# A three-branch scan backbone: each engine's queue put into the order of the kernel's own list schedule

## The chip, the core and the metric

The kernel runs on one core of one Trainium2 chip. The core has five engines with a queue each: TensorE (PE in the profile, its weight loads PEld), VectorE (DVE), ScalarE (ACT), GpSimd (POOL), and SyncE (SP), from whose queue every transfer between the device's memory and the core's own is issued here. An engine takes its instructions in the order in which they stand in its queue; an instruction that waits for a result holds up all that stand behind it. The metric is the device time of one execution in microseconds (us), lower is better.

## The reference

There are two layers over 256 context and 512 latent tokens of width 1024. Each layer projects the normed, modulated tokens once, runs three kinds of scan over them in both directions, and projects the joined results back:

```python
u_lat = rmsnorm(h_lat, norm_w[l]) * (1.0 + scale[:, None]) + shift[:, None]
...
(z_c, xbc_c, dt_c, q_c, k_c, v_c, gg_c, lr_c, u5_c, sg_c) = split_in_proj(u_ctx @ w_in[l])
(z_l, xbc_l, dt_l, q_l, k_l, v_l, gg_l, lr_l, u5_l, sg_l) = split_in_proj(u_lat @ w_in[l])
ssd_c, ssd_l = ssd_branch(...)
gla_c, gla_l = gla_branch(...)
s5_c, s5_l = s5_branch(...)
out_lat = jnp.concatenate([ssd_l, gla_l, s5_l], axis=-1) @ w_out[l]
h_lat = h_lat + gate[:, None] * out_lat
```

The SSD branch (16 heads, a convolution before it) and the GLA branch (4 heads) are linear-attention scans over chunks of 128 and 64 tokens; the S5 branch is a complex diagonal recurrence. Each runs forward and backward, context first, and hands its last state to the latent scan. The second layer gives out latent tokens alone.

## The kernel before

Everything lies channel by token: 128 channels on the partitions, up to 768 tokens along them. A projection of 128 output channels (`proj`, matmuls of L497 for the latent and L499 for the context tokens; `L691` for v) loads a weight block `wr`, splits it into a high part `wh` (ACT) and a low part `wl` (POOL, every third time DVE, L421), and sums 24 matmuls of 512 columns in a PSUM tile `pl` (and 24 of 256 columns in `pc`). The S5 output gate (L1008, L1010) and the output projection (L1044, L1046) are built alike. These matmuls, 5088 of the 6920, are called projections below; the others belong to the scans, norms and modulations.

The program is traced layer by layer in this order: modulation and norm; a small projection for dt and the decay of the scans; S5 input (`s5_in_maps` L351 to L359, matmuls L599), S5 recurrence on DVE (L631 to L634), S5 output (L672 to L674); q, k and v; the GLA heads (L765 to L793) and, in layer 0, the gate's share of the modulation (`mod_tiles`, L202); the gates (`spill_gate`, evicted by DVE at L516); GLA's norm (L808); twelve convolution tiles (`conv_tile`, L838 to L847); the SSD scan in six steps for each of two head groups; the z gates; the S5 output gate; `ssd_norm` (its first matmul is L955); the half of the output projection that takes GLA and S5 (`spilled_part`), and last the half that takes SSD.

An SSD step has three parts. `decay` loads rows of `acsD` into 128 partitions (L887, 1 MB) and makes the decay matrix with eight pairs of ACT and DVE instructions (L897 to L900); `within` multiplies it by the tokens (L908, L910); `between` carries the state: POOL weighs the tokens (L926) and decays the state (L936), PE makes the update (L931), DVE adds it (L937), and the part of the output that comes from the state is loaded for (L919), made (L917, L922) and added by POOL (L923). Each group has one work tile, `bA` or `bB`, so a load for the next step waits until the step before has read its rows.

Nothing in the kernel's text orders the engines. It is traced under `tile.TileContext(nc, schedule_with_timeline_sim=True)`: a scheduler goes through the traced instructions, gives out the buffers of the tile pools and sets the order of every queue, by the traced order as priority and durations from a model of its own.

Of the kernel before, what the change touches and what calls it, by code (L numbers as in the profile page):

```python
# [2 lines left out]

# [6 lines left out]
F32R = mybir.dt.float32r  # L10
# [27 lines left out]
STEPS = [(0, 1), (1, 0), (2, 5), (3, 4), (4, 3), (5, 2)]  # L38


@with_exitstack
def hybrid_backbone_kernel(
    ctx: ExitStack,
# [15 lines left out]
    V, S, G, PE = nc.vector, nc.scalar, nc.gpsimd, nc.tensor  # L59
# [8 lines left out]

    def T(tag, shape, bufs, dt=F32):
        uid[0] += 1  # L70
        return sb.tile(shape, dt, tag=tag, bufs=bufs, name=f"{tag}_{uid[0]}")

    def cv(n=NT):
        return T("cv", [128, NT], 3)[:, :n]

    def ev(n=NT):
        return T("ev", [128, 776], 2)[:, :n]

    def cs(n=1024):
        return T("cs", [128, 1024], 3)[:, :n]  # L80
# [13 lines left out]

    def m12():
        return T("m12", [128, 3072], 1)

    def ps(n=512, p=128):
        uid[0] += 1
        return psp.tile([128, 512], F32, tag="ps", bufs=3, name=f"ps_{uid[0]}")[:p, :n]  # L100
# [26 lines left out]
    def pcol(name, i=0, n=1):  # L127
        a = PAR[name][0] + i
        return P_[:, a : a + n]
# [351 lines left out]
    def layer(l, u):  # L481
# [216 lines left out]


        g4 = m12()  # L700
        gh = [g4[:, NT * i : NT * i + NT] for i in range(4)]
        wk = big("bB")
# [152 lines left out]
        def ssd_prep(g):  # L855

            if g == 0:
                t = m12()
                xtok = lambda c: t[:, 512 * c : 512 * c + 512]
            else:  # L860
                t = [cs() for _ in range(3)]
                xtok = lambda c: t[c // 2][:, 512 * (c % 2) : 512 * (c % 2) + 512]
            xts.append(xtok)
            for c in range(6):
                pt = ps()
                for i in range(4):
# [272 lines left out]
    hx, acc = layer(0, u)  # L1139
# [10 lines left out]
    hx, acc = layer(1, u)  # L1150
# [6 lines left out]
    for k in range(8):  # L1157
        o = hx[:, k, LC:NT]
        if k in POOL_FIN:
            G.tensor_tensor(o, o, rstd, MUL)  # L1160
        else:
            V.scalar_tensor_tensor(o, o, pcol("fnw", k), rstd, MUL, MUL)
        dma(outT[128 * k : 128 * k + 128], o)


def lay_out(np, x, c, ctx, c_ctx, norm_w, mod_w, mod_b, w_in, w_out, ssd_conv_w, ssd_conv_b, ssd_a_log,
# [77 lines left out]
```

## Time and profile before

| | |
|---|---|
| median of 3 runs | 1715.96 us (1715.52 to 1718.87) |
| profiled execution | 1718.59 us |
| its span, first to last instruction | 1716.9 us |
| busy: PE, DVE, ACT, POOL | 1415.7, 1209.7, 681.8, 596.5 us |
| mean granted TensorE clock | 0.906 of full |
| transfers | 234.42 MB, mean 137 GB/s |

Busy time is the time in which at least one instruction of an engine runs. Matmuls overlap, and where the clock is at the lower of its two levels the same work takes longer, so a busy PE is not a PE at full rate. [...]

### The profile page before, as it was taken

The numbers are of one execution on the slowest core, as the hardware profiler recorded it, in microseconds if no ns is written. First come the engines' busy times: TensorE is split into PE (matmuls) and PEld (weight loads), VectorE is DVE, ScalarE is ACT, GpSimd is POOL, SyncE is SP. The second block draws the span as 40 slices with busy tenths as digits, with TensorE's granted clock in tenths as the row PEclk, the third lists the DMA queues.
The fourth block names the chain that finished last, engine by engine and source line by source line (L and its number), as shares of the span: only waits on it lengthen the run. The fifth ranks groups of instructions, "written<-read, shape, count | busy, mean of one in ns | idle before, by whom it ended". The sixth has DMA issues, their size and how long they took to land.

```text
span 1716.9 us, 23372 instructions
## 1 busy us (share of the span) xinstructions
PE 1415.7 (82%) x8536; PEld 1141.4 (66%) x8536; DVE 1209.7 (70%) x2184; ACT 681.8 (40%) x1220; POOL 596.5 (35%) x492
## 2 busy tenths in 40 slices
PE   3879887787998988666899887996889888967786
PEld 1657776685877867455776655794679777745564
DVE  7957679824679778889913694559974986688742
ACT  3313242443335554544211241234254435545452
POOL 3201344312331244545222211144343232655454
PEclk8889998869998998888999988998988998988998
DMA  8564432246232235443485428722235333344542
GB/s 306 134 176 124 132 102 77 89 138 214 76 120 93 74 136 165 147 128 120 160 300 181 119 68 206 226 76 89 90 120 148 95 119 97 120 132 151 174 146 92
DMA packets 137147, 234.42 MB, mean 137 GB/s; under 512 B 31688, under 2 KB 72136, under 8 KB 137032
## 3 DMA queue, kind: packets, MB, share of 16 engines
q1 hardware_dynamic: 137032, 232.93, 43.9%
q8 instruction: 67, 1.10, 0.3%
q14 instruction: 48, 0.39, 0.1%
HBM read 188.25 MB, written 44.63 MB: 136 GB/s over the span
## 4 chain that ended last, share of the span: by engine, by line
DVE 32%; PE 28%; DMA 19%; issue 7%; ACT 6%; POOL 4%; SPq 1%; DVEq 0%; ACTq 0%; POOLq 0%
PE pl L497 7%; PE pl L1044 5%; DMA bB<-acsD 5%; DMA bc<-lpD 4%; PE pc L499 3%; DMA bA<-acsD 3%; DMA cs<-in_mod_w 3%; DVE xy L845 2%; PE pc L1046 2%; ACT bA L121 2%; DVE xy L633 2%; DVE xy L634 2%; PE pl L691 1%; DMA cs<-in_s5cb 1%; DVE bB L898 1%
## 5 line engine op out<-in xcount | busy, mean ns | idle before, releaser
L497 PE MATMUL pl<-hl,wh 128*128 128x512 f32 (+1 forms) x1184 | 409.5, 412 | 36.6 <-DVE ev L516 21.3
L421 POOL TENSOR_TENSOR wl<-wr,wh 128x1024 fp32r<-128x1024 f32 (+1 forms) x82 | 211.7, 2583 | 486.6 <-ACT wh L121 473.0
L497 PEld LDWEIGHTS pl<-hl,wh 128*128 128x128 f32 (+1 forms) x1184 | 225.4, 194 | 95.1 <-DVE ev L516 23.4
L497 PE MATMUL pl<-hl,wl 128*128 128x512 f32 (+1 forms) x592 | 241.7, 409 | 11.3 <-DVE wl L421 10.0
L121 ACT ACTIVATE wh<-wr 128x1024 fp32r<-128x1024 f32 (+1 forms) x122 | 127.7, 1046 | 236.4 <-PE pc L499 79.2
L499 PE MATMUL pc<-hl,wh 128*128 128x256 f32 (+1 forms) x864 | 211.5, 315 | 4.4 <-DVE ev L516 3.2
L499 PEld LDWEIGHTS pc<-hl,wh 128*128 128x128 f32 (+1 forms) x864 | 160.8, 212 | 20.5 <-issue 9.3
L497 PEld LDWEIGHTS pl<-hl,wl 128*128 128x128 f32 (+1 forms) x592 | 114.7, 194 | 40.0 <-DVE wl L421 11.1
L499 PE MATMUL pc<-hl,wl 128*128 128x256 f32 (+1 forms) x432 | 133.6, 310 | 0.0
L1044 PE MATMUL pl<-hl,wh 128*128 128x512 f32 x256 | 88.3, 421 | 15.8 <-ACT hl L121 4.6
L499 PEld LDWEIGHTS pc<-hl,wl 128*128 128x128 f32 (+1 forms) x432 | 90.9, 210 | 4.6 <-issue 3.2
L121 ACT ACTIVATE ev<-pl 128x512 f32<-128x512 f32 (+1 forms) x96 | 51.3, 534 | 94.7 <-PE pl L691 31.5
L121 ACT ACTIVATE bB<-bB 128x512 f32<-128x512 f32 (+4 forms) x40 | 45.7, 1143 | 98.0 <-DMA bB<-acsD 57.8
L845 DVE SCALAR_TENSOR_TENSOR xy<-ev,par_sb,xy 128x512 f32<-128x512 f32 (+1 forms) x112 | 81.6, 756 | 0.8
L691 PE MATMUL pl<-wh,hl 128*128 128x256 f32 x384 | 73.5, 291 | 0.0
L1044 PEld LDWEIGHTS pl<-hl,wh 128*128 128x128 f32 x256 | 50.4, 202 | 31.4 <-ACT hl L121 6.3
L691 PEld LDWEIGHTS pl<-wh,hl 128*128 128x128 f32 x384 | 61.1, 195 | 4.7 <-ACT bB L121 3.0
L421 DVE TENSOR_TENSOR wl<-wr,wh 128x1024 fp32r<-128x1024 f32 x40 | 54.5, 1361 | 11.4 <-ACT wh L121 11.2
L691 PE MATMUL pl<-wl,hl 128*128 128x256 f32 x192 | 55.3, 291 | 5.7 <-POOL wl L421 5.7
L1008 PE MATMUL pl<-hl,wh 128*128 128x512 f32 x128 | 48.2, 443 | 11.3 <-ACT cv L121 8.0
L1044 PE MATMUL pl<-hl,wl 128*128 128x512 f32 x128 | 53.2, 415 | 3.2 <-DVE wl L421 2.0
L121 ACT ACTIVATE bA<-bA 128x512 f32<-128x512 f32 (+2 forms) x30 | 23.5, 784 | 79.6 <-DMA bA<-acsD 59.1
(476 smaller groups left out, 3409.8 us busy)
## 6 DMA issues: line engine op xcount, KB each, us to landing
wr<-in_wblk SPq DMA_DIRECT2D x80, 512.0 KB
wr<-in_wout SPq DMA_DIRECT2D x32, 512.0 KB
hl<-in_mod_w SPq DMA_DIRECT2D x20, 512.0 KB
bA<-acsD SPq DMA_DIRECT2D x10, 1024.0 KB
bB<-acsD SPq DMA_DIRECT2D x10, 1024.0 KB
bc<-lpD SPq DMA_DIRECT2D x16, 512.0 KB
clD<-cs SPq DMA_DIRECT2D x64, 128.0 KB
cs<-clD SPq DMA_DIRECT2D x32, 256.0 KB
```

The lines of the kernel that those rows point to most:

```text
L121: return S.activation(out, in_, f, **kw)
L421: (eng or (V if wcount[0] % 3 == 0 else G)).tensor_tensor(wl, wr, wh.bitcast(F32), SUB)
L497: PE.matmul(p_l[:m], lhs, u[k][:, ui, LC:NT], start=st, stop=sp)
L499: PE.matmul(p_c[:m], lhs, u[k][:, ui, 0:LC], start=st, stop=sp)
L633: V.tensor_tensor(dst, dst, tr[:, 0, :n], ADD)
L634: V.tensor_tensor(dst, dst, tr[:, 1, :n], ADD)
L691: PE.matmul(p, u[k][:, ui, 128 * c : 128 * c + 128], ws[k // 4][wi][:, 256 * (k % 4) : 256 * (k % 4) + 256], start=n == 0, stop=n == 23)
L845: V.scalar_tensor_tensor(ac, raw[:, o + k : o + k + n], pcol("cw", w0 + k), ac, MUL, ADD)
L898: V.scalar_tensor_tensor(rf[:, h, :], rbw[:, h, :], rb[:, ih : ih + 1], rf[:, h, :], SUB, MIN)
L1008: PE.matmul(p_l, lhs, yg5[k][:, ui, LC:NT], start=n == 0, stop=n == 11)
L1044: PE.matmul(p_l, lhs, rhs[kk][:, ui, LC - t0 : NT - t0], start=st, stop=sp)
L1046: PE.matmul(p_c, lhs, rhs[kk][:, ui, 0:LC], start=st, stop=sp)
```

## The change

At the end of the trace the kernel calls a function of its own, `order_queues`. It makes a record for each traced instruction (`Step`): its queue, what it reads and writes, a duration from a formula for its engine and kind, and a lag until others may use the result. From the accesses it works out which instruction waits for which, and then goes through simulated time: whenever a queue is free, it takes the instruction that was traced first among those whose inputs have landed, if the pools have room for the tiles that it opens. It counts a DVE instruction with two streams from the core's memory and any POOL instruction but a memset as users of one port that only one may hold. At the end it adds an edge between each two neighbours of a queue, so that the scheduler that still runs afterwards has to keep this order. No instruction is added, removed or moved to another engine: both programs have the same 6920 matmuls, 748 transfers and 35 loads of ACT's function tables.

```diff
+    def cost(self):
...
+        if self.queue == "PE":
+            n, self.lag = cols(self.writes[0]), 150
+            if self.reads[0].dtype == F32R:
+                self.time = n * (0.443 if n >= 512 else 0.469)
+            else:
+                self.time = 2 * max(0.85 * n + 8, 118 if cols(self.reads[1]) > 64 else 75)
+        elif self.queue == "DVE":
+            scan = any(a.tensor.name.startswith("sm_") for a in self.reads)
+            self.time, self.lag = 60 + 2.28 * n if scan else ((120 if psum else 62) + n) / 0.96 + 25, 90
+            self.port = not psum and sum(cols(a) > 1 for a in self.reads) >= 2
+        elif self.queue == "Pool":
+            a, b = {"TensorTensor": (100, 2.18), "Memset": (90, 0.6), "TensorScalarPtr": (200, 1.6)}.get(self.kind, (150, 1.6))
+            self.time, self.lag, self.port = a + b * n, 120, self.kind != "Memset"
+        elif self.queue == "Activation":
+            self.time, self.lag = 120 + 0.88 * n, 120
...
+            rate = 190 if small >= 1024 else 120 if small >= 512 else 60
+            if any(s == 0 for s, _ in self.reads[0].ap):
+                rate = 95
+            self.time, self.lag, self.flow = 450, 2000, self.bytes / rate
...
+def order_queues(tc):
...
+    while count < len(steps):
...
+        for q in queues:
+            while free[q] <= now and heaps[q]:
+                skipped, s = [], None
+                while heaps[q] and len(skipped) < 60:
+                    n = heapq.heappop(heaps[q])
+                    if fits(steps[n]):
+                        if not (steps[n].port and port > now):
+                            s = steps[n]
+                            break
...
+    info = mybir.DependencyInfo(mybir.DependencyClass.NoSync, mybir.DependencyReason.DATA)
+    for q in queues:
+        for a, b in zip(done[q], done[q][1:]):
+            tc.add_manual_dep(b.ins, a.ins.name, info, reason="order of the queue")
...
         dma(outT[128 * k : 128 * k + 128], o)
+    order_queues(tc)
```

In the changed file a line of the kernel stands 197 lines lower: L497 is L694, L931 is L1128, and so on. Three places show how the orders differ.

PE, layer 1, SSD steps. `pl` is a z gate's projection; `ps` of L931 (L1128) is the update of an SSD state, `bA` and `bB` the two groups. Before, 24 projections and one transpose stand between the update into ps_11197 and the next one, into ps_11205; these are the last of them:

```order
L497 MATMUL pl_12073<-hl_8010,wl_12070 128x512
L497 MATMUL pl_12073<-hl_8015,wh_12069 128x512
L928 MATMUL pa_11249<-ident,bc_10753 128x128
L497 MATMUL pl_12073<-hl_8015,wh_12069 128x512
L497 MATMUL pl_12073<-hl_8015,wl_12070 128x512
L497 MATMUL pl_12073<-hl_8020,wh_12069 128x512 x2
L497 MATMUL pl_12073<-hl_8020,wl_12070 128x512
L497 MATMUL pl_12073<-hl_8025,wh_12069 128x512 x2
L497 MATMUL pl_12073<-hl_8025,wl_12070 128x512
L497 MATMUL pl_12073<-hl_8030,wh_12069 128x512 x2
L497 MATMUL pl_12073<-hl_8030,wl_12070 128x512
L931 MATMUL ps_11205<-bA_11163 128x512
```

In the changed order this is the whole stretch between the same two updates:

```order
L1128 MATMUL ps_11190<-bB_11164 128x512
L1128 MATMUL ps_11197<-bA_11163 128x512
L1125 MATMUL pa_11249<-ident,bc_10753 128x128
L694 MATMUL pl_11898<-hl_8030,wl_11895 128x512
L694 MATMUL pl_11933<-hl_7995,wh_11929 128x512
L1125 MATMUL pa_11257<-ident,bc_10753 128x128
L694 MATMUL pl_11933<-hl_7995,wh_11929 128x512
L694 MATMUL pl_11933<-hl_7995,wl_11930 128x512
L694 MATMUL pl_11933<-hl_8000,wh_11929 128x512 x2
L694 MATMUL pl_11933<-hl_8000,wl_11930 128x512
L1128 MATMUL ps_11205<-bA_11163 128x512
```

There are 7 projections between the two updates now, of gates that were traced earlier; the 24 of before stand further back.

POOL, the same steps. L926 and L936 are `between`'s, `wl` (L421) splits a weight block for a projection. Before:

```order
L936 TENSOR_TENSOR bB_11164<-bB_11164,dts_8183 128x512
L421 TENSOR_TENSOR wl_12070<-wr_12067,wh_12069 128x1024
L926 TENSOR_TENSOR bB_11164<-cs_11120,wf_8184 128x512
L926 TENSOR_TENSOR bA_11163<-m_1072_10656,wf_8184 128x512
L936 TENSOR_TENSOR bB_11164<-bB_11164,dts_8183 128x512
L926 TENSOR_TENSOR bA_11163<-m_1072_10656,wf_8184 128x512
L421 TENSOR_TENSOR wl_12160<-wr_12157,wh_12159 128x1024
L926 TENSOR_TENSOR bB_11164<-cs_11120,wf_8184 128x512
L421 TENSOR_TENSOR wl_12201<-wr_12198,wh_12200 128x1024
L926 TENSOR_TENSOR bB_11164<-cs_11121,wf_8184 128x512
```

After, at the end of the SSD steps:

```order
L1133 TENSOR_TENSOR bA_11163<-bA_11163,dts_8183 128x512
L1123 TENSOR_TENSOR bB_11164<-cs_11122,wf_8184 128x512
L618 TENSOR_TENSOR wl_12035<-wr_12032,wh_12034 128x1024
L618 TENSOR_TENSOR wl_12070<-wr_12067,wh_12069 128x1024
L1133 TENSOR_TENSOR bB_11164<-bB_11164,dts_8183 128x512
L1123 TENSOR_TENSOR bB_11164<-cs_11121,wf_8184 128x512
L1120 TENSOR_TENSOR xy_10216<-xy_10216,bB_11164 128x4x128 x2
L1133 TENSOR_TENSOR bB_11164<-bB_11164,dts_8183 128x512
L1120 TENSOR_TENSOR xy_10216<-xy_10216,bA_11163 128x4x128 x2
L1120 TENSOR_TENSOR xy_10216<-xy_10216,bB_11164 128x4x128 x2
L618 TENSOR_TENSOR wl_12160<-wr_12157,wh_12159 128x1024
L618 TENSOR_TENSOR wl_12201<-wr_12198,wh_12200 128x1024
```

The splits for two z gates (wl_12035, wl_12070) and for the S5 output gate (wl_12160, wl_12201), which stood among the first SSD steps, stand near the last ones or behind them.

PE, layer 1, S5 output (L672 to L674, tiles `pa`). Before, it stands among gate projections and a GLA head (L765):

```order
L497 MATMUL pl_10299<-hl_8020,wl_10296 128x512
L765 MATMUL ps_9629<-bB_9451,m_932_9450 128x128
L765 MATMUL ps_9630<-bB_9451,m_932_9450 128x128
L765 MATMUL ps_9629<-bB_9451,m_932_9450 128x128
L765 MATMUL ps_9630<-bB_9451,m_932_9450 128x128
L499 MATMUL pc_66<-hl_8020,wl_10296 128x256
L673 MATMUL pa_8740<-bA_8611,cs_8741 128x64
L673 MATMUL pa_8762<-bA_8611,cs_8763 128x64
L497 MATMUL pl_10299<-hl_8025,wh_10295 128x512
L499 MATMUL pc_66<-hl_8025,wh_10295 128x256
```

After:

```order
L694 MATMUL pl_9920<-hl_7995,wh_9916 128x512 x2
L694 MATMUL pl_9955<-hl_7995,wh_9951 128x512 x2
L869 MATMUL pa_8762<-bc_8474,cs_8763 128x64
L870 MATMUL pa_8740<-bA_8611,cs_8741 128x64
L870 MATMUL pa_8762<-bA_8611,cs_8763 128x64
L871 MATMUL pa_8740<-bA_8611,cs_8741 128x64
L869 MATMUL pa_8740<-bc_8474,cs_8741 128x64
L870 MATMUL pa_8740<-bA_8611,cs_8741 128x64
L871 MATMUL pa_8740<-bA_8611,cs_8741 128x64
```

The first S5 output tile of layer 1 has 3700 projections ahead of it instead of 3994, and the last one 3715 instead of 4039. Counts of the same kind over the program, projections that stand ahead of a landmark on PE:

| landmark on PE | before | after |
|---|---|---|
| layer 0, last S5 output matmul (L674) | 1064 | 763 |
| layer 0, GLA's norm (L808) | 1272 | 1104 |
| layer 0, first and last SSD update (L931) | 1809, 2160 | 1748, 2047 |
| layer 0, `ssd_norm` (L955) | 2256 | 2124 |
| layer 1, last S5 output matmul | 4039 | 3715 |
| layer 1, GLA's norm | 4224 | 3894 |
| layer 1, first and last SSD update | 4510, 4730 | 4445, 4567 |
| layer 1, `ssd_norm` | 4826 | 4644 |
| end | 5088 | 5088 |

## Rows read from the trace of the kernel before

**Rows 1.** The page: span, busy time by engine, granted clock in 40 slices.

```profile
span 1716.9 us, 23372 instructions
PE 1415.7 (82%) x8536; PEld 1141.4 (66%) x8536; DVE 1209.7 (70%) x2184; ACT 681.8 (40%) x1220; POOL 596.5 (35%) x492
PEclk8889998869998998888999988998988998988998
```

**Rows 2.** The page: the chain that ended last, by engine and by line.

```profile
DVE 32%; PE 28%; DMA 19%; issue 7%; ACT 6%; POOL 4%; SPq 1%; DVEq 0%; ACTq 0%; POOLq 0%
PE pl L497 7%; PE pl L1044 5%; DMA bB<-acsD 5%; DMA bc<-lpD 4%; PE pc L499 3%; DMA bA<-acsD 3%; DMA cs<-in_mod_w 3%; DVE xy L845 2%; PE pc L1046 2%; ACT bA L121 2%; DVE xy L633 2%; DVE xy L634 2%; PE pl L691 1%; DMA cs<-in_s5cb 1%; DVE bB L898 1%
```

**Rows 3.** Waits of PE: line and releaser, us in total, times, longest.

```profile
PE pa L202 <- DMA cs<-in_mod_w: 21.6, 7, 7.0
PE pl L497 <- DVE ev L516: 21.3, 5, 11.4
...
PE pl L497 <- ACT wh L121: 12.3, 4, 5.3
PE pl L497 <- DVE wl L421: 10.0, 3, 9.2
...
PE ps L931 <- DVE bA L937: 6.5, 2, 3.4
```

**Rows 4.** The chain at the SSD update shown above: start, us, what.

```profile
1474.77 1.72 PE ps L931 x4
1476.48 3.00 PE pl L497 x13
1479.48 0.11 PE pa L928
1479.59 2.54 PE pl L497 x11
1482.13 0.86 PE ps L931 x2
```

**Rows 5.** The chain from 1460 to 1629 us, layer 1's SSD steps, by line.

```profile
by line: DMA bA<-acsD 15.9%; DMA bB<-acsD 14.8%; PE pl L497 10.8%; DMA cv<-h1D 7.2%; DVE bB L898 6.3%; DMA cs<-zD 5.8%; issue 5.5%; DVE bA L900 5.4%; PE ps L931 4.1%; ACT bB L121 2.7%; DVE xy L950 1.9%; DVE bB L900 1.9%; ACT hl L121 1.6%; D
```

**Rows 6.** The chain at the end of the program: the last projections.

```profile
1659.60 4.39 PE pl L1044 x18
1666.38 32.50 PE pl L1044 x142
```

**Rows 7.** Stretches: busy us of each engine (instructions), granted clock, transfer share, GB/s.

```profile
320.00:440.00 120.00, 95.62 (x677) 82.67 (x677) 46.18 (x85) 55.07 (x62) 21.62 (x32) 0.80 0.53 162
1240.00:1320.00 80.00, 71.84 (x470) 64.21 (x471) 45.46 (x81) 38.78 (x39) 25.05 (x32) 0.85 0.47 135
1120.00:1160.00 40.00, 40.00 (x305) 36.26 (x305) 22.28 (x35) 14.29 (x30) 21.48 (x27) 1.00 0.21 63
...
604.00:811.00 207.00, 154.32 (x880) 121.02 (x876) 179.10 (x313) 109.07 (x251) 104.34 (x68) 0.88 0.44 142
1460.00:1629.00 169.00, 133.64 (x647) 97.19 (x646) 128.95 (x212) 81.25 (x191) 95.12 (x65) 0.92 0.45 142
811.00:983.00 172.00, 156.48 (x1022) 122.27 (x1022) 91.52 (x205) 38.66 (x60) 45.17 (x20) 0.97 0.56 187
320.00:360.00 40.00, 27.49 (x185) 24.37 (x183) 25.08 (x44) 29.68 (x20) 7.28 (x10) 0.74 0.30 92
720.00:760.00 40.00, 28.34 (x159) 21.74 (x159) 33.57 (x53) 19.69 (x48) 19.88 (x13) 0.76 0.42 127
```

**Rows 8.** The chain from 395 to 430 us: by line, and its longest piece.

```profile
by line: DMA cs<-in_mod_w 66.4%; PE pa L202 9.4%; DVE cv L748 8.9%; PE pc L499 8.4%; PE pl L497 6.7%; PE ps L790 2.1%; PE ps L779 1.1%; DVE ev L516 1.0%; SPq L517 0.9%; issue 0.8%; SPq L229 0.0%
...
409.97 18.31 DMA cs<-in_mod_w
```

**Rows 9.** Waits of ACT for the loads of `acsD`.

```profile
ACT bA L121 <- DMA bA<-acsD: 63.5, 18, 7.2
ACT bB L121 <- DMA bB<-acsD: 60.7, 18, 6.0
```

More of the change, by code (lines that the diff above doesn't have):

```diff
@@ L1 @@
+import heapq
 import math
@@ L38, with spans @@
 STEPS = [(0, 1), (1, 0), (2, 5), (3, 4), (4, 3), (5, 2)]
+BUFS = {}
+def spans(a):
+    t, off, ap = a.tensor, a.offset, [(int(s), int(n)) for s, n in a.ap]
+    if t.space == bass.MemoryType.DRAM:
+        unit, p0, p1 = 64, 0, 1
+    else:
+        width = math.prod(t.shape[1:])
+        unit, p0, off = 1, off // width, off % width
+        p1 = p0 + ap[0][1]
+        ap = ap[1:]
+    runs = [(off, off)]
+    for s, n in sorted(ap, key=lambda d: abs(d[0])) if unit > 1 else ap[::-1]:
+        if n == 1 or s == 0:
+            continue
+        if len(runs) == 1 and abs(s) <= max(unit, runs[0][1] - runs[0][0] + 1):
+            far = s * (n - 1)
+            runs = [(runs[0][0] + min(far, 0), runs[0][1] + max(far, 0))]
+        else:
+            runs = [(lo + s * i, hi + s * i) for lo, hi in runs for i in range(n)]
+    bits = 0
+    for lo, hi in runs:
+        bits |= ((1 << (hi // unit - lo // unit + 1)) - 1) << (lo // unit)
+    return p0, p1, bits
@@ new lines, with __init__, piece @@
+class Step:
+    TABLES = {"Exp": 1, "Ln": 1, "Tanh": 2, "Gelu_apprx_tanh": 3}
+    def __init__(self, n, i):
+        self.n, self.ins, self.kind = n, i, type(i).__name__[4:]
+        self.queue = str(i.engine).split(".")[-1]
+        self.reads, self.writes = ([x.bass_ap for x in side if getattr(x, "bass_ap", None) is not None]
+                                   for side in (i.ins, i.outs))
+        self.port, self.table, self.bytes, self.flow = False, 0, 0, 0.0
+        self.cost()
+    def cost(self):
+        both = self.reads + self.writes
+        cols = lambda a: math.prod(n for _, n in list(a.ap)[1:])
+        n = max(map(cols, both), default=1)
+        psum = any(a.tensor.space == bass.MemoryType.PSUM for a in both)
+        if self.queue == "PE":
+            n, self.lag = cols(self.writes[0]), 150
+            if self.reads[0].dtype == F32R:
+                self.time = n * (0.443 if n >= 512 else 0.469)
+            else:
+                self.time = 2 * max(0.85 * n + 8, 118 if cols(self.reads[1]) > 64 else 75)
[8 more added lines that the diff above has]
+            self.time, self.lag = 120 + 0.88 * n, 120
+            self.table = self.TABLES.get(str(self.ins.func).split(".")[-1], 0)
+        else:
+            size = lambda a: 4 * math.prod(n for _, n in a.ap)
+            self.bytes = max(map(size, both))
+            def piece(a):
+                if a.tensor.space != bass.MemoryType.DRAM:
+                    return 1 << 20
+                r = 1
+                for s, n in list(a.ap)[::-1]:
+                    if s != r:
+                        break
+                    r *= n
+                return 4 * r
+            small = min(map(piece, both))
+            rate = 190 if small >= 1024 else 120 if small >= 512 else 60
+            if any(s == 0 for s, _ in self.reads[0].ap):
+                rate = 95
+            self.time, self.lag, self.flow = 450, 2000, self.bytes / rate
@@ L70, in T @@
         uid[0] += 1
+        BUFS[tag] = bufs
         return sb.tile(shape, dt, tag=tag, bufs=bufs, name=f"{tag}_{uid[0]}")
@@ L96, in m12 @@
         return T("m12", [128, 3072], 1)
+    BUFS.update(ps=3, pa=2, pl=2)
     def ps(n=512, p=128):
```

87 lines of the change are left out of this document (added).

## The prediction

> **What bounds the kernel now.** The page comes first. PE is busy for 1415.7 of 1716.9 us, DVE for 1209.7, POOL and ACT for far less, and no transfer queue is near its limit [rows 1]. PE's 301 idle us are what an order can win at most through PE alone; its mean clock of 0.906 is a second loss, and it falls in the same places. The chain that ended last says that no single engine is the bound: DVE has 32% of it, PE 28%, transfers 19%, and the largest line, the projections of L497, has 7% [rows 2]. So the kernel alternates. In some stretches the scan chains on DVE, ACT and POOL decide, and PE fills in with projections; in others PE has a queue of projections and the scans wait. The stretches show it: in the SSD steps of layer 0 DVE is busy for 179 of 207 us and PE for 154; in those of layer 1, 129 and 134 of 169; but from 320 to 440 us, where S5 output and GLA run, DVE has 46 of 120 and PE 96, and from 1240 to 1320 DVE has 45 and PE 72 of 80 [rows 7]. PE's own waits are many and short, by the gates' eviction, the weight split, the modulation's loads and the SSD state alike [rows 3].
>
> **What the change does to this.** Work is the same; only orders differ. The landmark table shows the direction: nearly every scan matmul has fewer projections ahead of it, 168 fewer at layer 0's GLA norm, 330 fewer at layer 1's, 182 fewer at layer 1's `ssd_norm`. A projection that does not stand ahead of a scan must stand behind it. So the change is a trade: filler is taken out of the scans' way and done later, and it pays if the scans become shorter by more than the filler then costs.
>
> **What it costs.** (a) The end of layer 1. Behind its `ssd_norm` stand 444 projections instead of 262. All are of 512 columns, and the last 142 of them took 32.50 us on the chain, 0.229 each [rows 6]. The 182 more cost 41.7 us, and nothing covers them, for after `ssd_norm` only projections are left: +42. (b) The end of layer 0. 132 more projections stand between its `ssd_norm` and layer 1's norm. They are the S5 output gate's, 60 of 512 columns and 72 of 256, which count half: 60 x 0.229 + 72 x 0.115 = 22.0. PE is busy there for 156 of 172 us at a clock of 0.97 [rows 7], so nothing can hide them but the 16 idle us. I take +22, bounds +6 and +22.
>
> **What it wins.** The scans' stretches can shrink only as far as the engine that carries them is idle in them; DVE's idle time is therefore the bound of each term.
>
> (c) SSD steps of layer 1, 1460 to 1629 us. DVE idles for 40 of 169 us. On the chain there, projections (L497) hold 10.8%, which is 18 us, and a load for the output projection (cv from h1D), for which DVE's queue stood still with SSD work behind, another 7.2%, 12 us [rows 5]. One such place is whole in the rows: between two state updates the chain goes through 13 and 11 projections, 5.5 us [rows 4], and the new order has 7 there instead of 24. The steps hold 122 projections instead of 220, and the weight splits on POOL go behind. Those two items give -30, bounds 0 and -40.
>
> (d) SSD steps of layer 0: DVE idles for 28 of 207 us. ACT stands still for the 1 MB loads of `acsD` for 124 us in 36 waits over both layers [rows 9], in its queue's order, while its next instructions belong to the other group. The new order knows such a load as some 13 us and can put the other group first. But the load itself stays, with one work tile per group. The filler here hardly shrinks (299 instead of 351 projections). Two thirds of the idle time: -18, bounds 0 and -28.
>
> (e) GLA and S5 output of layer 1, 1240 to 1320 us: DVE idles for 34.5 of 80 us while PE has projections among the S5 output [rows 7]; the new order has 324 fewer ahead of its end. Two thirds: -22, bounds 0 and -35.
>
> (f) The same in layer 0, 320 to 440 us: DVE idles for 74 of 120, PE for 24. But two thirds of the chain from 395 to 430 us is a load of the modulation weights [rows 8], which needs bandwidth and not order, though it starts earlier if the S5 output before it ends earlier. I take -30, bounds 0 and -74.
>
> (g) PE's waits at projections while scans stood behind them. I matched PE's instructions of the trace one by one with the two orders. At 43 waits, 98 us, the new order has more matmuls ahead of the one waited for. The largest have rows: 21.3 for the gates' eviction, 12.3 and 10.0 for weight splits [rows 3]. Whether the matmuls put ahead are ready then depends on how early the scans are; by the times of before, 25 of the 98 us had one. -25, bounds 0 and -98.
>
> **Sum.** The profiled run took 1718.6 us, 1.7 more than its span. 1718.6 + 42 + 22 - 30 - 18 - 22 - 30 - 25 = 1655.6. The median of before lies 2.6 us under the profiled run, so 1653 by the median; I forecast **1655**.
>
> **One rule against it.** Where PE idles for about a third of a stretch the granted clock is down: 0.74 at 27.5 busy us of 40, 0.76 at 28.3 of 40, and 1.00 at 40.0 of 40 [rows 7]. Fewer projections in the scans may leave PE emptier there. In the two SSD stages PE is busy for 288 us at clocks of 0.88 and 0.92. If both fell to 0.76, the busy times would grow to 179 and 162 us, 53 us more, of which perhaps half lies on the chain: +26, and the forecast would be 1681. [...]
>
> **The rivals.**
> Slower: the scans are not limited by what stands around them but by their own latencies and loads. For it speaks that on the chain of layer 1's SSD steps the `acsD` loads alone hold 30.7%, 52 us [rows 5], and that PE waited for the SSD state already with more projections ahead [rows 3]; with fewer it would only wait longer. Then (a) and (b) stay and (c) to (g) are nothing: 1718.6 + 64 = 1783; with a third of the gains, 41, it is 1741. It decides from the point where the stages (c) to (g) together shrink by less than 64 us. Against it: DVE idles for 177 us in (c) to (f), a little over a third of which would do. Chance 0.22, at 1720 to 1783.
>
> No difference: the gains and the deferred filler cancel within a few us. Nothing holds them together, so 0.06, at 1712 to 1719.
>
> Larger gain: the waits of PE at projections go altogether, as scans stand ready (g at -80), and (f) reaches -50: 1655 - 55 - 20 = 1580. For it speaks that each stage starts earlier than the one before it assumed; against it that the modulation's loads do not shrink. Chance 0.15, at 1550 to 1600.
>
> Clock: as above, 1680 to 1710. Chance 0.12.
>
> That the change does nothing is excluded: 380 of PE's 6922 places hold the same instruction as before.
>
> **How the numbers follow.** The forecast has 0.45, between 1600 and 1700. The range leaves out half of the larger gain's cases and a little over half of the slower rival's: 1590 to 1735, with 0.06 below and 0.13 above. Faster is forecast, larger gain and clock, 0.72; same 0.06; slower 0.22. The bound for these is 0.2%, 3.4 us, about what runs of this kernel can tell from no change.
>
> **What would show it.** Right: the first S5 output and GLA matmuls come earlier in both layers; the SSD steps of layer 1 take 140 us or less from the first state update to `ssd_norm`, with DVE over 85% busy; the tail from there to the end grows from 89 to about 130 us, nearly all projections at a clock near 1; PE's idle time falls from 301 towards 240 us. Wrong: the SSD steps take as long as before with PE below 70%, the `acsD` loads keep their 60 us of ACT waits each, or the clock falls below 0.85 in the scans; and, for the larger gain, L497's waits gone from the table.

## The result, and the profile after

The changed kernel takes 1851.15 us (median of 4 runs, 1844.81 to 1853.98) against 1717.39 for the kernel before beside it: ratio 1.0774, 95% interval 1.0742 to 1.0806. It is 134 us slower, where 1655 us, 61 us faster, had been forecast.

The page of the changed kernel, its span, its busy times and the clock line (tenths of full speed in 40 slices):

```profile
span 1843.1 us, 23427 instructions
PE 1439.1 (78%) x8536; PEld 1147.2 (62%) x8536; DVE 1193.4 (65%) x2184; ACT 683.8 (37%) x1220; POOL 572.4 (31%) x492
PEclk8799877889889988878989998995689899888998
```

Every engine does the work of before [rows 1], spread over 126 us more: PE idles for 404 us instead of 301.

The stages show where. I cut both traces at the same instructions: the first matmul of GLA's norm, the first SSD state update, the first of `ssd_norm`, and layer 1's first norm; the last stage ends where the last output transfer is issued, some 4 us before the end of the span. Length is in us; "proj." counts the projections that start in the stage.

| stage | before | proj. | after | proj. | change |
|---|---|---|---|---|---|
| layer 0 to GLA's norm | 472.4 | 1272 | 468.3 | 1104 | -4.1 |
| convolutions, layer 0 | 123.4 | 537 | 151.9 | 644 | +28.5 |
| SSD steps, layer 0 | 195.0 | 447 | 196.8 | 376 | +1.8 |
| to layer 1's norm | 191.6 | 768 | 248.7 | 900 | +57.1 |
| layer 1 to GLA's norm | 395.2 | 1200 | 351.8 | 870 | -43.4 |
| convolutions, layer 1 | 82.4 | 286 | 131.3 | 551 | +48.9 |
| SSD steps, layer 1 | 168.5 | 316 | 154.5 | 199 | -14.0 |
| to the end | 84.0 | 262 | 135.7 | 444 | +51.7 |

The four stages with scans lost 686 projections and became 59.7 us shorter. The four others got these 686 and became 186.2 us longer. The difference is the result.

Busy times of the changed kernel in those eight stages and in two pieces of the S5 stretches, rounded to whole us:

```profile
core 0: us, PE busy (x) PEld busy (x) DVE busy (x) ACT busy (x) POOL busy (x), PEclk, DMA share, GB/s
0.00:468.00 468.00, 342.95 (x2461) 275.87 (x2462) 291.40 (x650) 150.67 (x239) 105.83 (x110) 0.87 0.46 140
468.00:620.00 152.00, 132.91 (x718) 111.34 (x716) 116.36 (x174) 68.95 (x123) 44.08 (x66) 0.93 0.23 79
620.00:817.00 197.00, 145.99 (x806) 112.58 (x806) 151.79 (x286) 95.42 (x246) 86.91 (x62) 0.84 0.39 131
817.00:1066.00 249.00, 206.37 (x1285) 158.96 (x1286) 142.30 (x294) 64.36 (x94) 72.37 (x28) 0.91 0.50 162
1066.00:1417.00 351.00, 275.73 (x1675) 228.99 (x1675) 223.34 (x391) 122.46 (x175) 81.18 (x76) 0.83 0.40 120
1417.00:1549.00 132.00, 118.98 (x619) 98.33 (x618) 102.07 (x140) 57.85 (x100) 43.01 (x62) 0.94 0.25 84
1549.00:1703.00 154.00, 106.73 (x527) 75.48 (x527) 109.40 (x197) 72.35 (x182) 79.05 (x58) 0.84 0.36 117
1703.00:1843.00 140.00, 109.44 (x452) 85.63 (x452) 56.73 (x58) 51.77 (x64) 60.03 (x31) 0.93 0.39 137
240.00:280.00 40.00, 10.77 (x82) 9.96 (x81) 38.94 (x47) 6.76 (x10) 1.19 (x2) 0.67 0.20 56
1240.00:1280.00 40.00, 10.68 (x68) 9.43 (x68) 33.05 (x34) 20.88 (x12) 5.84 (x6) 0.63 0.21 63
```

Read the rows of the SSD steps (620 and 1549) against [rows 7]: DVE, which in layer 1 was to become over 85% busy, has 77% and 71%, PE 74% and 69%. Nobody is full. In the last two rows DVE goes through the S5 recurrence, PE has 11 of 40 us, and POOL 1 and 6.

Why PE has nothing there is seen at a weight block. ACT makes `wh`, POOL then makes `wl`, and only then may all of a projection's matmuls run. ACT and POOL of the changed kernel in the SSD steps of layer 1 (start in us, duration in us, instruction):

```profile
1556.73 1.06 ACT L318 ACTIVATE wh<-wr 128x1024 fp32r<-128x1024 f32 x1 [0.81 <-PE pl L694]
...
1585.80 1.10 POOL L1133 TENSOR_TENSOR bB<-bB,dts 128x512 f32<-128x512 f32 x1
1586.86 1.10 POOL L1123 TENSOR_TENSOR bA<-m,wf 128x512 f32<-128x512 f32 x1
1589.76 1.06 POOL L1123 TENSOR_TENSOR bB<-cs,wf 128x512 f32<-128x512 f32 x1 [1.80 <-PE ps L1128]
1590.78 2.35 POOL L618 TENSOR_TENSOR wl<-wr,wh 128x1024 fp32r<-128x1024 f32 x1
```

`wh` was ready at 1557.8; the split came 33 us later, behind some 20 instructions of the scan, with idle time among them: its place in POOL's queue held it, not POOL's speed. PE over that time:

```profile
1576.39 0.71 PE L694 MATMUL pl<-hl,wh 128*128 128x512 f32 x2
1579.15 0.33 PE L1125 MATMUL pa<-ident,bc 128*128 128x128 f32 x1 [2.05 <-DVE bB L1090]
...
1587.50 0.47 PE L1125 MATMUL pa<-ident,bc 128*128 128x128 f32 x1 [5.34 <-DVE bA L1090]
1587.77 1.91 PE L1128 MATMUL ps<-bB 128*128 128x512 f32 x2
...
1595.72 0.33 PE L1125 MATMUL pa<-ident,bc 128*128 128x128 f32 x1 [1.03 <-ACT bB L318]
1595.80 0.48 PE L694 MATMUL pl<-hl,wl 128*128 128x512 f32 x1
```

From 1577.1 to 1595.8 there is no projection, while PE waits 5.3 us for DVE at one place; the first to come again uses a `wl`. The S5 stretch of layer 0 shows it more sharply:

```profile
279.79 0.21 POOL L843 MEMSET bA<- 64x64 f32 x1 [32.60 <-DVE xy L831]
...
281.15 0.71 PE L869 MATMUL pa<-bc,cs 128*128 128x96 f32 x2 [29.74 <-DMA cs<-gD]
...
284.57 2.36 POOL L618 TENSOR_TENSOR wl<-wr,wh 128x1024 fp32r<-128x1024 f32 x1
```

ACT has a `wh` ready at 248.9, POOL stands idle for 32.6 us because the next instruction of its queue waits for DVE's recurrence, and the split, six places behind, starts at 284.6, 35.7 us after its `wh`. PE stands still for 29.7 us meanwhile: its next instruction, of the S5 output, waits for a load, and no projection stands ahead of it. Of all 122 splits, the time from the end of `wh` to the start of `wl` adds up to 174 us before (longest 21.6) and 454 after (longest 43.4).

### The profile page after: what moved, and what is told of

Read it like the earlier page. It is cut to its first block, busy times and chain, and to the rows that moved or that the text cites. A ratio compares the mean times of both kernels' runs of the same rounds, so it can differ in the third digit from the quotient of the medians.

```text
span 1843.1 us, 23427 instructions
## 1 busy us (share of the span) xinstructions
PE 1439.1 (78%) x8536; PEld 1147.2 (62%) x8536; DVE 1193.4 (65%) x2184; ACT 683.8 (37%) x1220; POOL 572.4 (31%) x492
## 5 line engine op out<-in xcount | busy, mean ns | idle before, releaser
L694 PE MATMUL pl<-hl,wh 128*128 128x512 f32 (+1 forms) x1184 | 443.3, 422 | 23.2 <-DVE ev L713 9.0
L618 POOL TENSOR_TENSOR wl<-wr,wh 128x1024 fp32r<-128x1024 f32 (+1 forms) x82 | 205.1, 2504 | 498.6 <-ACT wh L318 467.5
L694 PEld LDWEIGHTS pl<-hl,wh 128*128 128x128 f32 (+1 forms) x1184 | 231.7, 200 | 82.0 <-DVE ev L713 9.8
L696 PE MATMUL pc<-hl,wh 128*128 128x256 f32 (+1 forms) x864 | 241.5, 303 | 32.9 <-ACT ev L318 22.9
L694 PE MATMUL pl<-hl,wl 128*128 128x512 f32 (+1 forms) x592 | 250.6, 424 | 12.5 <-DVE wl L618 9.5
L694 PEld LDWEIGHTS pl<-hl,wl 128*128 128x128 f32 (+1 forms) x592 | 118.0, 199 | 46.9 <-DVE wl L618 10.9
L1042 DVE SCALAR_TENSOR_TENSOR xy<-ev,par_sb,xy 128x256 f32<-128x256 f32 (+1 forms) x112 | 75.1, 727 | 0.6
L618 DVE TENSOR_TENSOR wl<-wr,wh 128x1024 fp32r<-128x1024 f32 x40 | 48.8, 1219 | 38.2 <-ACT wh L318 38.2
L869 PE MATMUL pa<-bc,cs 128*128 128x96 f32 (+1 forms) x128 | 32.5, 345 | 50.4 <-DMA cs<-gD 50.1
L1205 PE MATMUL pl<-hl,wh 128*128 128x512 f32 x128 | 48.9, 450 | 29.0 <-DVE hl L1193 9.8
L1241 PEld LDWEIGHTS pl<-hl,wh 128*128 128x128 f32 x256 | 48.9, 194 | 29.1 <-DVE hl L623 7.6
L1095 DVE SCALAR_TENSOR_TENSOR bA<-bA,dts 128x128 f32<-128x128 f32 x80 | 39.9, 560 | 40.6 <-ACT bA L318 40.6
L966 DVE SCALAR_TENSOR_TENSOR bB<-bB,dcs,ps 64x128 f32<-64x128 f32 x88 | 29.9, 340 | 50.2 <-PE ps L962 47.6
```

The source lines that it names most:

```text
L618: (eng or (V if wcount[0] % 3 == 0 else G)).tensor_tensor(wl, wr, wh.bitcast(F32), SUB)
L694: PE.matmul(p_l[:m], lhs, u[k][:, ui, LC:NT], start=st, stop=sp)
L696: PE.matmul(p_c[:m], lhs, u[k][:, ui, 0:LC], start=st, stop=sp)
L869: PE.matmul(o, tt[:, gg * 128 : gg * 128 + 128], ug(g)[:, c0:96], start=True, stop=False)
L966: V.scalar_tensor_tensor(sp[lo_, i + 1, :], sp[lo_, i, :], dcs[lo_, i : i + 1], upd(lo_, i), MUL, ADD)
L1042: V.scalar_tensor_tensor(ac, raw[:, o + k : o + k + n], pcol("cw", w0 + k), ac, MUL, ADD)
```

## The experiments

Times are medians in us, with the ratio to the kernel before run beside them. "Feed" is the number of projections in the four stages with scans: 3235 of 5088 before, 2549 after. thin, half and two_loads are edits of the kernel before, and thin and half leave out work; the others are edits of the changed kernel.

**Which queue's order.** pe_only adds the edges to PE's queue alone, not_pe (`queues[1:]`) to the four others:

```diff
-    for q in queues:
+    for q in ("PE",):
         for a, b in zip(done[q], done[q][1:]):
```

> Only PE's queue is held to the list schedule; DVE, ACT, POOL and SP are ordered by the scheduler again. Theory 1 (the loss is PE's order: projections are taken out of the scans' gaps and run where nothing covers them): the loss stays, 1810 to 1870 us. Theory 2 (the loss is in the other queues, where loads and DVE work stand in an order that is right only at the plan's durations): most of it goes, 1700 to 1760 us.

> DVE, ACT, POOL and SP are held to the list schedule, PE is not. Theory 1 (PE's order): the loss goes, 1690 to 1740 us. Theory 2 (the other queues' orders): it stays, 1800 to 1870 us.

Measured: 1978.27 (1.1536) and 1922.38 (1.1219). Neither theory: each half of the order alone is worse than the whole. Feed is 2549 and 2448, so both halves keep the projections out of the scans: PE's because it is the same order, the other four probably because they hold the splits. The delay of the splits, counted as above, is 147 us in pe_only and 544 in not_pe. So with PE held to its order the splits need not be late for the loss to stay: late splits matter in the plan too, which then gives PE an order with few projections in the scans.

**Durations of the plan.** loads changes two prices:

```diff
-            rate = 190 if small >= 1024 else 120 if small >= 512 else 60
+            rate = 65 if self.bytes >= 1 << 19 and small >= 1024 else 190 if small >= 1024 else 120 if small >= 512 else 60
-                rate = 95
+                rate = 95 if self.reads[0].ap[0][0] == 0 else 28
```

> All five queues are held, but the plan prices two kinds of load as the trace shows them: the acsD rows for the state's output (5.2 us in the plan, a median of 12 in the trace) and the 512 KB weight blocks (5.2 against 15). Theory 3 (the plan's gaps in the scans are too short because loads are too cheap in it, so too few projections are put into them): the SSD stages lose 10 to 20 us each and some 60 to 100 us of the 134 come back, 1750 to 1790 us. Theory 1 or 2 with a cause other than loads: 1830 to 1870 us.

refit has these and

```diff
-                self.time = n * (0.443 if n >= 512 else 0.469)
+                self.time = n * (0.47 if n >= 512 else 0.53)
-                self.time = 2 * max(0.85 * n + 8, 118 if cols(self.reads[1]) > 64 else 75)
+                self.time = 0.85 * n + 8
+            if self.kind == "TensorScalarPtr" and not scan and (self.port or n == 128):
+                self.time += 40 if self.port else 90
-            self.time, self.lag = 120 + 0.88 * n, 120
+            self.time, self.lag = 292 if n == 128 else 120 + 0.88 * n, 120
```

> As the run before, and DVE's and ACT's short instructions 40 to 90 ns dearer, the 512-column matmuls at 0.47 ns a column and the small float32 matmuls at half of the plan's price. Theory 3 in its wide form (wrong durations of every kind): 1690 to 1740 us. If only the loads matter: as the run before, within 15 us. If durations are not the cause: over 1800 us.

Measured: 1838.94 (1.0715) and 1819.43 (1.0615). Theory 3 in this form fell: 12 us, an interval that touches that of the changed kernel, and 32. The delay of the splits grew, to 554 and 712 us (longest 95.5), as it would in a plan whose scans take longer while the splits stand behind them.

**The splits first.** The heap's key becomes a rank:

```diff
+    rank = [s.n - 5000 * (s.queue in ("DVE", "Pool", "Activation") and any(tag(t) in ("wh", "wl") for t in s.tiles)) for s in steps]
-            heapq.heappush(heaps[steps[n].queue], n)
+            heapq.heappush(heaps[steps[n].queue], (rank[n], n))
```

> The list schedule as it is, but ACT, DVE and POOL take a weight block's split (wh, wl) before any other work that is ready. Theory 4 (the projections are missing from the scans because their own splits, traced later than the scan's work, stand behind it on POOL and DVE): a split again follows its wh within some 5 us instead of up to 39, PE's idle time in the SSD steps and the S5 stretch falls, and 60 to 130 of the 134 us come back, 1720 to 1790 us. Theory 3 (durations): the splits only take time from the scans, 1830 us or more.

Measured: 1769.04 (1.0311), 82 us less. The split shown above stands here; columns as there:

```profile
1470.82 1.06 ACT L319 ACTIVATE wh<-wr 128x1024 fp32r<-128x1024 f32 x1 [0.81 <-PE pl L695]
...
1473.76 2.41 POOL L619 TENSOR_TENSOR wl<-wr,wh 128x1024 fp32r<-128x1024 f32 x1
1476.13 1.12 POOL L1134 TENSOR_TENSOR bB<-bB,dts 128x512 f32<-128x512 f32 x1
```

It waits 1.9 us instead of 33; over all splits the delay is 47 us, the longest 5.1. Feed is 2691. Theory 4 stands, for about 60% of the loss.

s_dve adds the DVE and ACT lines of refit.

> As the run before, with DVE's and ACT's short instructions 40 to 90 ns dearer in the plan. If durations matter once the splits are out of the way: 10 to 40 us below the run before. If not: within 10 us of it.

Measured: 1744.99 (1.0162), 24 us less: with the splits out of the way, the same prices help.

**The port.** no_port lets the plan start any instruction whose engine is free; split_no_port does that with the splits first.

```diff
-                        if not (steps[n].port and port > now):
+                        if True:
```

> The list schedule as it is, but the plan knows no port that DVE and POOL share: an instruction of either starts when its engine is free. Theory 5 (the plan's rule starves POOL, since DVE is asked first whenever the port comes free, and POOL's splits are late for that reason): 1740 to 1800 us. If the rule prices something real and is not what delays the splits: 1830 to 1870 us.

> The weight splits first, and no shared port of DVE and POOL in the plan. If the port's rule prices something real, the plan now packs POOL's splits beside DVE's work and both run late on the chip: 1810 to 1860 us. If the rule is itself a part of the loss: below 1769 us, the time of the splits first with the rule.

Measured: 1847.45 (1.0766), no different from the changed kernel, and 1837.42 (1.0711), 68 us above split_first. The rule prices something real. It does delay splits (263 us of delay without it instead of 454), but the time does not follow them; where the difference is lost was not looked for.

**All that feeds PE.** feed_only extends the rank's tags to `("wh", "wl", "hl", "cv")`.

> The list schedule at its own prices, but ACT, DVE and POOL take whatever feeds a projection before other ready work: the splits of weights (wh, wl) and of tokens (hl), and the work on the tiles between them (cv). Theory 4 (PE's filler starves behind scan work on the other engines): at or below the run with the weight splits alone, 1735 to 1775 us, with more of the S5 gate's projections ahead of layer 0's ssd_norm than 60.

Measured: 1759.97 (1.026); 108 S5 gate projections ahead of layer 0's `ssd_norm`, feed 2764. Not separated from split_first by its interval (1.0211 to 1.031 against 1.0269 to 1.0353).

feed_prices has this and

```diff
-                self.time = 2 * max(0.85 * n + 8, 118 if cols(self.reads[1]) > 64 else 75)
+                self.time = 1.2 * max(0.85 * n + 8, 118 if cols(self.reads[1]) > 64 else 75)
+            if self.kind == "TensorScalarPtr" and not scan and (self.port or n == 128):
+                self.time += 20 if self.port else 90
-            rate = 190 if small >= 1024 else 120 if small >= 512 else 60
+            rate = 130 if small >= 1024 and self.bytes >= 1 << 19 else 190 if small >= 1024 else 120 if small >= 512 else 60
-                rate = 95
-            self.time, self.lag, self.flow = 450, 2000, self.bytes / rate
+                rate = 95 if self.reads[0].ap[0][0] == 0 else 60
+            self.time, self.lag, self.flow = 450, 2500, self.bytes / rate
```

and in the rank `- 200 * (s.queue == "PE" and any(tag(t) in ("wh", "wl") for t in s.tiles))`.

> As feed_only, and the plan's prices moved towards the trace: small float32 matmuls at 0.6 of the plan's price, two-stream DVE instructions 20 ns dearer, the acsD rows for the state's output and the 512 KB loads slower, 0.5 us more until a load may be used; and PE takes a projection ahead of work traced up to 200 instructions before it. Theory 4 with theory 3 as its second half (prices matter once the feed is free): 1640 to 1700 us, faster than before. If prices don't matter even then: 1735 to 1775 us.

Measured: 1683.48, ratio 0.9805 (0.9776 to 0.9834): faster than both kernels, than the one before by 2%. Feed is 3253, a little above the kernel before. Its SSD steps of layer 0, the stretch behind them, the SSD steps of layer 1 and the end, columns as in the stages above:

```profile
566.00:783.00 217.00, 169.77 (x968) 133.18 (x967) 168.61 (x301) 115.37 (x271) 102.79 (x68) 0.89 0.40 133
783.00:961.00 178.00, 171.75 (x1059) 126.66 (x1060) 113.95 (x248) 47.17 (x71) 52.59 (x22) 0.98 0.59 195
...
1408.00:1596.00 188.00, 155.66 (x739) 114.20 (x739) 133.99 (x217) 89.55 (x203) 96.10 (x67) 0.92 0.44 146
1596.00:1682.00 86.00, 59.01 (x224) 43.71 (x222) 34.03 (x37) 33.94 (x44) 36.83 (x21) 0.84 0.30 103
```

It does the opposite of what the forecast valued. Its SSD steps are 22 and 19 us longer than before, with 538 and 410 projections instead of 447 and 316. What stands behind those of layer 0 falls from 191.6 to 178 us; the stages ahead of the SSD steps, 1073.4 us together before, take 1013. There its gain on the kernel before lies, and the feed, which is about the same, does not explain it.

**What the scans take without filler.** thin keeps the first and the last matmul of each projection:

```diff
             for n, (k, wi, ui) in enumerate(seq):
                 st, sp = n == 0, n == 23
+                if 0 < n < 23:
+                    continue
```

and the same at the other three places; half skips `if n % 2 and n != 23`.

> The kernel before with 2 of each 24 (of 12 in the S5 gate) projection matmuls; all loads, splits, evictions and scans stay. The other matmuls are left out, so its time is that of the scans and of all that feeds the projections. Rival of the prediction (the scans are bound by their own latencies and loads): the SSD steps of layer 1 still take over 140 of 168.5 us, those of layer 0 over 165 of 195. The prediction's own view (projections stand in the scans' way): 130 us or less and 160 or less.

> The kernel before with 13 of each 24 projection matmuls (7 of 12 in the S5 gate); the others are left out, so the output is not the reference's. In the run with 2 of 24 PE's clock was down to 0.61, which may have stretched the scans; here it should lie higher, near 0.75. If projections in the SSD steps cost them nothing: 160 us or more in layer 1, 185 or more in layer 0, and the clock was not what held the other run up. If they are in the way and only the low clock hid it: 150 and 175 or less.

Measured, one run each: 1537.39 and 1560.35 us, set against the trace of the kernel before shown so far (its one run beside half took 7178 us and is not used). The SSD steps of both layers, thin and then half:

```profile
521.00:738.00 217.00, 108.30 (x563) 68.72 (x562) 168.66 (x313) 107.19 (x248) 108.37 (x70) 0.72 0.58 193
1296.00:1472.00 176.00, 88.64 (x371) 54.42 (x370) 140.58 (x214) 85.66 (x195) 104.01 (x68) 0.70 0.51 163
```

```profile
540.00:737.00 197.00, 141.33 (x737) 107.32 (x736) 176.21 (x287) 106.32 (x250) 105.83 (x67) 0.81 0.50 161
1322.00:1483.00 161.00, 109.98 (x518) 78.55 (x517) 134.99 (x212) 84.70 (x199) 96.65 (x65) 0.84 0.48 151
```

With half of the filler gone they take 197 and 161 us, where they took 195 and 168.5. With all but a twelfth gone, 217 and 176, at a clock of about 0.7, so that run alone would not tell; the other, at 0.81 and 0.84, does. The scans of the SSD steps set their own length, and the projections that the kernel before has among them cost next to nothing. That has a bound: feed_prices has 91 and 94 more there, and its steps are longer by 0.24 and 0.20 us for each, about a projection's full time; whether the projections or the rest of its order do that was not separated. To GLA's norm nothing is won in layer 1 (409 us in both, 395 before), but some in layer 0 (426 and 411, 472 before). What shrinks most in half is the stretch behind layer 0's SSD steps, 191.6 to 112.4; the convolutions and the end give 40 us together.

**What of feed_prices does it.** prices_alone has its prices without the rank, feed_fp32 the rank of feed_only with the small float32 price alone, feed_late all but the 200.

> feed_prices without its order of the feed: only the plan's prices are changed, every engine again takes what was traced first. If prices are a cause of their own: 1730 to 1790 us. If they count only where the feed of PE goes first: 1800 to 1850 us, near the two runs with dearer loads and refitted prices.

> feed_only with one price changed: the small float32 matmuls of the scans at 0.6 of the plan's. If the plan left projections out of the scans because it thought PE full of the scans' own matmuls: 1710 to 1735 us, and more than 259 projections in layer 1's SSD steps. If this price does not matter: 1750 to 1765 us.

> feed_prices without its last rule: PE takes what was traced first, and no projection ahead of it. If projections cost the scans next to nothing where they stand ahead of them, taking the rule away costs 15 us or more, 1700 to 1730 us, and more projections stand behind layer 1's ssd_norm than 216. If they are in the scans' way: at or below 1683 us.

Measured: 1767.70 (1.0304), 1722.45 (1.0045), 1694.03 (0.9866, 0.9822 to 0.9909). Prices alone win 83 us, the feed alone 91, both 157: two causes of similar size that nearly add. Prices alone did better than expected, although the delay of the splits is 626 us there. The small matmuls' price, one number, is worth 38 us on top of the feed, with 436 projections in layer 1's SSD steps instead of 259. The last rule is not settled: its intervals touch, and 192 projections stand behind `ssd_norm` without it, not more than 216.

All orders of the same work side by side, by feed:

| kernel | feed | us | | kernel | feed | us |
|---|---|---|---|---|---|---|
| not_pe | 2448 | 1922 | | split_first | 2691 | 1769 |
| no_port | 2543 | 1847 | | s_dve | 2762 | 1745 |
| after | 2549 | 1851 | | feed_only | 2764 | 1760 |
| pe_only | 2549 | 1978 | | feed_fp32 | 3079 | 1722 |
| loads | 2564 | 1839 | | feed_late | 3220 | 1694 |
| split_no_port | 2595 | 1837 | | before | 3235 | 1717 |
| refit | 2605 | 1819 | | feed_prices | 3253 | 1683 |
| prices_alone | 2609 | 1768 | | | | |

From after to feed_prices it is 168 us for 704 projections. Of these 458 have 512 columns and 246 have 256; at 0.229 [rows 6] and half of that (18 of 256 columns took 2.16 us on the chain of before at 587.77 us, 0.12 each) their whole time would be 133 us. So the table fits the view that a projection outside the scans' stages costs its whole time, without showing it, and the feed is not all: at 2543 to 2609 the times spread over 210 us.

**What sets the length of the SSD steps.** two_loads makes each of the 36 loads for the state's output in two halves:

```diff
-                        dma(ep[d], bass.AP(tensor=acsD[l].tensor, offset=acsD[l][cc, d, 8 * g].offset,
-                                           ap=[[512, 2], [0, 64], [1, 512]]))
+                        for x in range(2):
+                            dma(ep[d][64 * x : 64 * x + 64],
+                                bass.AP(tensor=acsD[l].tensor, offset=acsD[l][cc, d, 8 * g].offset + 512 * x,
+                                        ap=[[0, 64], [1, 512]]))
```

> The kernel before with each load of acsD rows for the state's output (L919: 2 x 64 rows of 512, with the 2 outermost) made as two loads of 64 rows. The SSD steps did not get shorter when half of the projections were left out, so something of their own sets their length. If it is these loads (a median of 12 us from issue to use), and their outermost dimension of 2 is what makes them slow, they fall to 4 to 7 us, the SSD steps of both layers to 150 to 180 and 125 to 155 us, and the time to 1650 to 1700. If the loads are as long as before, or other work sets the length: 1710 to 1720 us.

> feed_prices with the same two loads. If its SSD steps too are set by these loads: 1600 to 1665 us. If its projections, now 948 in the SSD steps, fill them: 1675 to 1690 us.

Measured: 1677.37 (0.9782, 0.9737 to 0.9827) and 1640.47 (0.955, 0.9518 to 0.9582). Where ACT waited for such a load, its work started a median of 10.2 us after the issue before (30 waits), and 3.4 in two_loads, counted from the half that came last (9). ACT's waits for `acsD` in two_loads, 124 us in [rows 9], and its SSD steps (waits: us in all, times, longest; stretches as above):

```profile
ACT bA L121 <- DMA bA<-acsD: 12.4, 6, 3.6
...
ACT bB L121 <- DMA bB<-acsD: 6.0, 7, 1.5
```

```profile
592.00:765.00 173.00, 140.24 (x830) 108.86 (x829) 161.74 (x277) 97.54 (x239) 95.90 (x64) 0.91 0.48 152
1430.00:1584.00 154.00, 127.51 (x647) 93.86 (x645) 136.70 (x212) 81.55 (x192) 98.64 (x65) 0.96 0.49 158
```

The steps are 22 and 15 us shorter, and DVE is busy for 93% and 89% of them. The order was left to the scheduler as before; with 36 more transfers it came out a little different (401 and 315 projections in the SSD steps instead of 447 and 316), so layer 1, with the same filler, is the cleaner case. feed_prices gains 43 us by it, so the best order and the shorter loads add, and that kernel is 78 us faster than the one before. The traces show the difference. The 128 packets of 2 KB of one such load run about two at a time before and take 5.4 to 6.2 us (three loads between 646 and 670 us); the two halves run up to 12 to 17 at a time and take 1.6 to 2.7 us (nine pairs between 622 and 687 us of two_loads). The count of packets under 512 B changes too, before and in two_loads:

```profile
DMA packets 137147, 234.42 MB, mean 137 GB/s; under 512 B 31688, under 2 KB 72136, under 8 KB 137032
...
DMA packets 138228, 234.43 MB, mean 140 GB/s; under 512 B 32768, under 2 KB 73216, under 8 KB 138112
```

They are 1080 more. Before, two packets of 4 B stand at the end of each of the three loads (652.33 and 652.46 us, 661.40 and 661.47, 669.64 and 669.81). With two for each of the 36, and the other transfers' as before, the 72 halves would have 1080 + 72 = 1152, 16 each: an estimate from these counts. The edit changes the outermost size of a load, 2 to 64, and the number of loads; which of the two makes the packets run closer together was not separated.

## Why the prediction was wrong

The trade was named rightly: filler out of the scans, done later, and it pays if the scans shrink by more. Both sides of the sum were wrong. (Its terms add up to 1657.6 and not to 1655.6; less 2.6 for the median that is the 1655 forecast.)

The cost was counted at two places of four. The forecast had read that 168 projections fewer stand ahead of layer 0's GLA norm and 330 fewer ahead of layer 1's, and then charged only those still left at the two `ssd_norm`. The rest fell due between: 107 and 265 more in the convolution stages, +28.5 and +48.9 us. This is the step that failed first; no term, and no rival, held it. That alone turns 64 us of cost into 141.

(a) +42 for the end: +51.7 measured, for the 182 projections forecast. (b) +22, with +22 as the upper bound: +57.1 for the 132 forecast. The filler fell due there as forecast, but not at PE's pace. In the stretch of (b) PE idles for 43 of 249 us and is busy 206 at a clock of 0.91, where it was busy 156 of 172 at 0.97 [rows 7]. Cut where the S5 gate ends and the output projection begins, it is:

```profile
817.00:865.70 48.70, 31.90 (x140) 26.30 (x140) 45.97 (x71) 28.13 (x31) 23.27 (x9) 0.82 0.22 75
865.70:1065.70 200.00, 174.18 (x1144) 132.39 (x1144) 96.02 (x225) 35.98 (x64) 49.10 (x19) 0.93 0.56 184
```

The gate's 132 projections take 48.7 us and not 22: DVE is busy for 46.0 of them and PE for 31.9, and PE's largest wait in the whole stretch is for the gate's product by DVE (12.6 us in 2 waits). The output projection takes 200 us, where the stage before took 191.6 in all. The bound of +22 took PE to be full and counted PE's time alone.

(c) -30: -14.0. (d) -18: +1.8. (e) and (f), -52 together: the two stages to GLA's norm changed by -47.5, so the sum was about right, but 43 of it lies in layer 1 and 4 in layer 0. In layer 0 S5's last output matmul comes 61 us earlier (336.4 instead of 397.7), and the 75 us of filler and scan behind it then take 132. (g) -25, the waits at projections: PE's idle time grew by 103 us. Of the 125 us forecast, 60 came.

What failed under (c) to (f) is one premise: that a stretch can shrink as far as DVE is idle in it. The runs with half and a twelfth of the filler show that the SSD steps do not. What held them was in the rows and read wrongly: (d) put ACT's 124 us in 36 waits [rows 9] down to the 1 MB loads for the decay, and asked of an order to work around them. By the shapes of the waiting instructions 30 of the 36 waits, with 117 of the 124 us, are before the exponential of the state's output, which reads one of the 36 loads of 256 KB; six, with 7 us, go by the 1 MB loads. With the small loads alone made shorter 106 of the 124 us are gone. The changed order left most of it, 102 us; ACT's waits in it:

```profile
ACT bB L318 <- DMA bB<-acsD: 66.3, 15, 7.8
...
ACT bA L318 <- DMA bA<-acsD: 35.6, 12, 7.2
```

The slower rival had this mechanism, at a chance of 0.22, and was right in it; its time, at most 1783, was too low because it shared the missing cost. The clock was a smaller part than its rival said: 0.877 over the span, 0.84 in both SSD stages, not 0.76. The traces of before and after hold two levels of it, 1.0 and 0.5 of full, and the figure of a stretch is their mean over its time. What lowers the clock stays open. It was 0.67 and 0.63 where PE stood at 11 of 40 us, but the reading that it falls where PE idles for a third came from chosen slices: from 680 to 720 us the kernel before has 27.3 busy us of 40 at 0.99. And the lower level, 0.50, was also granted where the profile has PE busy throughout, with S5's small output matmuls and GLA's in turn:

```profile
1300.00:1330.00 30.00, 30.00 (x155) 28.00 (x155) 7.70 (x23) 5.70 (x9) 0.78 (x4) 0.50 0.41 114
```

In the kernel before such matmuls ran at 1.00 (1300 to 1310 us, 88 of them). So the kind of matmul alone does not set the level.

Behind it stands a reason that the order itself showed and the forecast passed over: that the splits on POOL had moved behind the scan was read as relief for the scan. It was the filler's feed that went.

## What to carry to other kernels

When a schedule moves filler, follow the count of filler at every landmark to the end of the program; a piece that leaves a latency-bound stretch can cost its full time or more somewhere else, and the stretch may give little back; a run without the filler shows which, and also says where to look instead, here at a load of 256 KB whose packets ran two at a time. A list schedule that takes what was traced first can starve the work that prepares the filler for another engine; give that preparation the higher rank. And a price in such a plan is worth what it does to the order: the small matmuls' price moved the time by 38 us, while two loads priced nearer to the trace moved it by 12.

## What the runs showed of the hardware

With 46% of the projections' matmuls left out 156 us go, with the next 46% only 23, while the mean granted clock falls from 0.80 to 0.61: beyond the first half, PE's largest work is almost wholly hidden.

DVE's instructions take longer beside POOL's work also where the plan counts them as free of the port. In the changed kernel's trace the first instruction of a convolution (L838 in the kernel before, one stream from memory, 256 columns) takes 0.40 to 0.47 us in the 13 cases in which POOL is idle or clears memory as it starts, and 1.39 to 2.48 in the 7 in which POOL is at other work; a decay instruction with two streams (L898) has a mean of 0.36 in 121 cases and 1.26 in 39.

Eight small float32 matmuls of `within`, two passes each, took 1.09 us at one place of the changed kernel and 1.98 at another:

```profile
1574.45 1.09 PE L1105 MATMUL ps<-bA,m 128*64 128x128 f32 x16
...
1589.61 1.98 PE L1105 MATMUL ps<-bB,cs 128*64 128x128 f32 x16
```

That is 0.14 and 0.25 us each, at a granted clock of 1.00 (1574 to 1576 us) and 0.50 (1587 to 1592 us, behind 5.3 idle us); the plan says 0.234. So the plan's price is about that of the lower clock.
